# Feed-forward input in even-odd order, and norm factors moved into layer 1's key, value and query weights

## The chip, the core and the metric

One core of a Trainium2 chip runs the whole program. The metric is the device time of one execution in microseconds (us); the core's span in the profile is given beside it where both are known. TensorE (PE, and PEld for its weight loads) does the matmuls, VectorE (DVE) and ScalarE (ACT) the elementwise work, GpSimd (POOL) a little of it, and SyncE (SP) issues nearly all transfers.

## The reference

A trunk of two layers on 256 tokens of 1024 features, all in float32: layer 0 has attention over 16 heads, layer 1 has windowed attention with sinks over 16 query heads and 4 shared key/value heads, and each layer ends in a gated feed-forward block with a causal convolution of width 3. What the change touches, cut from the reference:

```python
def rmsnorm(x, g):
    y = x * rsqrt(mean(x * x, axis=-1) + EPS)
    return y * g
...
hk = rmsnorm(x, kv_norm)                       # layer 1
k, v = split(hk @ w_kv_b, 2)
h = rmsnorm(x, attn_norm[1])
q = partial_rope(heads(h @ w_q_b))
...
def conv_ffn(h, w_up, conv_w, conv_b, w_down): # both layers, h = rmsnorm(x, ffn_norm[l])
    u = h @ w_up                               # 1024 -> 2 * 2816
    u = conv_b + sum(conv_w[j] * shifted(u, j) for j in range(3))
    gate, val = split(u, 2)
    return (silu(gate) * val) @ w_down
```

A norm has two kinds of factors: one per token (the inverse root) and one per feature (`g`). The per-feature factor may stand at the input or at the rows of the weight matrix; the product is the same up to rounding.

## The kernel before

Tokens lie in two blocks of 128 (`b`), features in 8 chunks of 128 (`c`), which come in two halves of four (`n`). Every float32 operand of a projection is split in two parts: a rounded high part and the low part that is left. A product is then three matmuls: high x high, high x low, low x high.

**Weights.** They come in 92 units of 128 x 2048 numbers (1 MB each), in the order of their use. `fetch` loads a unit into one of three buffers `wr`; `prepare` splits it piece by piece: `hi_part` copies a piece to `wh` on ScalarE (L164), `lo_part` subtracts on VectorE and writes `wl` (L167). There are four buffers each of `wh` and `wl`, so unit i+4 is prepared when unit i has been used (`used`), and unit i+3 is fetched when unit i is split. The number of pieces `n` is 2 for most units (1024 wide) and 4 for some. Units 49 and 50 hold layer 1's key and value weights (`U_KV`), 51 to 54 its query weights (`U_QB`, each all 8 chunks of 256 columns), 55 on its output weights, 16 to 37 and 59 to 80 the two up projections.

**Order.** `chain` puts off small steps by an amount of planned time and `tick` runs those that are due while matmuls are written down; `require` runs what a matmul needs. From that order a list scheduler sets the order on each engine, except in stretches marked by hand.

**Features.** `feats` turns one block and half of the residual `xr` from tokens x features to features x tokens: four transposes on TensorE (L271) into two PSUM banks `t`, then per pair of chunks two ScalarE copies with the per-feature factor as scale (L283), a VectorE cast to the high part (L286) and a subtraction for the low part (L287). There are only two `t` banks, shared with other transposes. For the feed-forward block the scaled copy is kept as `y` (`keep`), because the per-token factors come later: the first four units of the up projection use the unscaled input and are scaled afterwards, while `scale_x` multiplies `y` by the row `rb` of token factors (L732) and splits it again (L734, L735) for the other 18 units. Between the layers (`after_f0`) `feats` makes two sets from the same transposes, `kT_h` with `kv_norm` and `qT_h` with `attn_norm[1]`, each with its own copies, casts and subtractions.

**Projections.** The up projection (L719 to L721) holds 128 x 128 weights and streams 256 tokens of one chunk; per unit it does 2 halves x 8 chunks x 3 products, for 22 units a layer. `proj` (L324 to L326) does it the other way round: it holds a block's features and streams weight columns, 512 for keys and values, 256 for queries. Its weights are packed on the host so that columns 0, 2, 4, ... of a group stand first and 1, 3, 5, ... behind, and a matmul reads them alternately from both halves:

```python
def turns(ap):
    return ap.rearrange("p (a t) -> p t a", a=2)
def pairs(ap):
    return ap.rearrange("p (t a) -> p t a", a=2)
...
nc.tensor.matmul(pairs(o), xh[:, blk(b)], turns(wh), start=(c == 0), stop=False)
```

After a projection of keys or queries, `rotate` copies the sums out with the token factor (L1046 for keys, L1059 for queries), applies the rotary embedding on VectorE (`rope`, L353 to L359), transposes on TensorE (L365) and splits the result (L376, L371). The attention then computes scores (L490 to L497).

Of the kernel before, what the change touches and what calls it, by code (L numbers as in the profile page):

```python
# [14 lines left out]
P = 128  # L15
# [45 lines left out]
def trunk(ctx: ExitStack, tc, x, xw, pos, cpk, fin, sinks, w, out):  # L61
# [96 lines left out]
    def fetch(i):  # L158
        if i < N_UNITS:
            raws[i] = wp.tile([P, UNIT], F32, tag="raw", name=f"wr{i}", bufs=3)  # L160
            nc.sync.dma_start(raws[i], w[i])

    def hi_part(i, c):
        nc.scalar.activation(wq[i][0][:, c], raws[i][:, c], AF.Copy)  # L164

    def lo_part(i, c):
        nc.vector.tensor_tensor(out=wq[i][1][:, c], in0=raws[i][:, c], in1=f(wq[i][0][:, c]), op=ALU.subtract)  # L167

# [4 lines left out]
    def prepare(i):  # L173

        if i >= N_UNITS:
            return
        n = 4 if i <= 5 or 1 <= i - U_UP0 <= 3 or 1 <= i - U_UP1 <= 3 or U_QB + 1 <= i <= U_OB else 2
        cut = [slice(k * UNIT // n, (k + 1) * UNIT // n) for k in range(n)]
# [84 lines left out]
    def new_hT():  # L263

        return [(quad(), quad()) for _ in range(2)]

    def feats(b, n, sets, key, keep=None):

# [6 lines left out]
        def steps(hT, g, y, m):  # L275
            c = slice(2 * m, 2 * m + 2)
            hi, lo = (part[:, c, blk(b)] for part in hT[n])
            y_ = y[:, c]

            def gain():  # L280
                for j in range(2):
                    col = g + 4 * n + 2 * m + j
                    nc.scalar.activation(y_[:, j], ts[m][:, j * P:(j + 1) * P], AF.Copy, scale=cp[:, col:col + 1])  # L283

            def parts():
                nc.vector.tensor_copy(hi, y_)  # L286
                nc.vector.tensor_tensor(out=lo, in0=y_, in1=f(hi), op=ALU.subtract)  # L287

            return gain, parts

        for k, (hT, g) in enumerate(sets):
            y = mid().rearrange("p (j t) -> p j t", j=4) if keep is None else keep[n][:, :, blk(b)]
            for m in range(2):
                gain, parts = steps(hT, g, y, m)
                chain(key, (200.0 + 1000.0 * k + 500.0 * m, gain), (500.0, parts))

    def square(b, n):
# [402 lines left out]
    def ffn(layer, u_up, u_dn, hT, y, rb, after, tail=None):  # L700
# [5 lines left out]
        def mm(i, up, cs_):  # L706
            need(u_up + i)
            hi, lo = wq[u_up + i]
            for j in range(2):
                o = up[j]  # L710
                for c in cs_:
# [5 lines left out]
                    s_ = slice((2 * c + j) * P, (2 * c + j + 1) * P)  # L717
                    xh, xl = hx(hT if i < n_raw else hS, c)
                    nc.tensor.matmul(o, hi[:, s_], xh, start=(c == 0), stop=False)  # L719
                    nc.tensor.matmul(o, hi[:, s_], xl, start=False, stop=False)  # L720
                    nc.tensor.matmul(o, lo[:, s_], xh, start=False, stop=(c == KC - 1))  # L721
                    tick(3 * 256 / 2.4)

        def scale_x(m):
# [4 lines left out]
            def times():  # L729
                for b in range(NB):  # L730
                    require("rb", b)
                nc.vector.tensor_tensor(out=y_, in0=y_, in1=rb.unsqueeze(1).to_broadcast([P, 2, S]), op=ALU.mult)  # L732

# [295 lines left out]
    o_down[0].finish(3, after_a, by_half=True)  # L1029
    kT_h = new_hT()  # L1030
    qT_h = new_hT()
    rs1 = []

    def after_f0(b, n):
        chain(("sq", b), (3000.0, lambda: square(b, n)))
        if n == 1:
            chain(("rs", b), (3000.0 + 700.0, lambda: rs1.append(rstd_of(b))))
        feats(b, n, [(kT_h, G_KV), (qT_h, G_ATTN1)], ("x", b, n))

# [10 lines left out]
    for b in range(NB):  # L1050
        o = bank("acc")
        run(proj(o, kT_h, b, cols512(U_KV), (U_KV, U_KV + 1) if b else ()))
        rotate(o, 2, b, kT[:, 0:2], kT[:, 2:4], ("qk", 0), lambda t, b=b, o=o: kv_out(t, b, o),
# [7 lines left out]
    def q_group(g):  # L1061
        q = quad()
        for b in range(NB):
            o = bank("acc")[:, :256]
            yield from proj(o, qT_h, b, cols256(U_QB + g), (U_QB + g,) if b else ())
            rotate(o, 2, b, q[:, 0:2], q[:, 2:4], ("qk", g), lambda t, b=b, o=o: q_out(t, b, o))
# [167 lines left out]
```

## Time and profile before

| | |
|---|---|
| three timed runs | 564.3, 564.4 and 563.48 us, median 564.3 |
| profiled execution | 563.05 us, its span 561.2 us |
| layer 0 | up projection from 116 to 238 us, down projection to 296 us |
| layer 1 | keys and values from 296 us, first queries from 308 us, scores from 318 us |
| layer 1's feed-forward block | up projection from 376 to 498 us, down projection to 553 us |

The profile lists each engine's busy time, idle times with what ended them, and the chain of work that ended last. A matmul's recorded duration overlaps that of its neighbours, so rates are read from starts.

### The profile page before, as it was taken

How to read it: one execution, taken by the hardware profiler on the slowest of the kernel's cores; microseconds unless marked ns; L12 is line 12 of the kernel's file. 1: busy time of each engine (PE TensorE's matmuls, PEld its weight loads, DVE VectorE, ACT ScalarE, POOL GpSimd, SP SyncE). 2: the span in 40 equal slices, each digit the busy share in tenths (PEclk: the TensorE clock that was granted, in tenths of full speed). 3: DMA queues.
4: the chain of work that ended last, by engine and by line, in shares of the span. 5: the costliest groups of instructions: out<-in, count | busy, mean ns of one | idle time of the engine just before them, and what ended most of it. 6: DMA issues, size and time to landing. Idle time of an engine off the chain costs nothing.

```text
span 561.2 us, 10529 instructions
## 1 busy us (share of the span) xinstructions
PE 548.0 (98%) x4022; PEld 510.9 (91%) x4022; DVE 439.1 (78%) x932; ACT 377.0 (67%) x767; POOL 107.3 (19%) x130
## 2 busy tenths in 40 slices
PE   9998999999999999999999999999999999999995
PEld 8997898899999999988888988889999999998884
DVE  6899988589798888764369988888898888874514
ACT  6759887779567777644349798887657777663313
POOL 8422202011422332100001000001332322210003
PEclk9999999999999999999999999999999999999998
DMA  8954464432466665566542724242465565656301
GB/s 320 375 200 171 151 227 149 151 131 96 161 221 221 226 223 193 192 222 220 203 172 88 289 76 151 75 151 76 151 221 204 200 211 217 239 205 224 121 0 75
DMA packets 15312, 101.00 MB, mean 180 GB/s; under 512 B 1952, under 2 KB 2080, under 8 KB 3744
## 3 DMA queue, kind: packets, MB, share of 16 engines
q1 hardware_dynamic: 14976, 100.09, 50.2%
q8 instruction: 31, 0.51, 0.4%
q10 hardware_dynamic: 288, 0.26, 0.1%
q14 instruction: 17, 0.14, 0.1%
HBM read 99.30 MB, written 1.05 MB: 179 GB/s over the span
## 4 chain that ended last, share of the span: by engine, by line
PE 81%; DVE 9%; ACT 4%; DMA 3%; issue 2%; POOL 0%; SPq 0%; DVEq 0%; POOLq 0%; ACTq 0%
PE acc L624 9%; PE acc L625 9%; PE acc L629 9%; PE u L721 6%; PE u L719 6%; PE u L720 6%; PE t L721 6%; PE t L719 6%; PE t L720 6%; DVE wl L167 4%; PE acc L720 2%; PE acc L719 2%; PE acc L721 2%; PE t L574 2%; DMA wr<-in_w 2%
## 5 line engine op out<-in xcount | busy, mean ns | idle before, releaser
L167 DVE TENSOR_TENSOR wl<-wr,wh 128x1024 fp32r<-128x1024 f32 (+1 forms) x208 | 223.4, 1090 | 59.6 <-ACT wh L164 59.0
L164 ACT ACTIVATE wh<-wr 128x1024 fp32r<-128x1024 f32 (+1 forms) x204 | 187.4, 951 | 62.6 <-PE acc L629 49.0
L763 POOL TENSOR_TENSOR m<-m,m 128x256 f32<-128x256 f32 x44 | 63.7, 1448 | 177.2 <-DVE m L758 126.1
L624 PE MATMUL acc<-wh,q 128*128 128x512 f32 x238 | 92.1, 387 | 0.0
L625 PE MATMUL acc<-wl,q 128*128 128x512 f32 x238 | 90.6, 380 | 0.0
L719 PE MATMUL u<-q,wh 128*128 128x256 f32 x320 | 88.4, 277 | 0.0
L720 PE MATMUL u<-q,wh 128*128 128x256 f32 x320 | 88.1, 276 | 0.0
L721 PE MATMUL u<-q,wl 128*128 128x256 f32 x320 | 88.0, 275 | 0.0
L721 PE MATMUL t<-q,wl 128*128 128x256 f32 x288 | 79.2, 275 | 0.0
L719 PE MATMUL t<-q,wh 128*128 128x256 f32 x288 | 79.2, 275 | 0.0
L720 PE MATMUL t<-q,wh 128*128 128x256 f32 x288 | 79.2, 275 | 0.0
L629 PE MATMUL acc<-wh,q 128*128 128x512 f32 x238 | 74.6, 379 | 0.0
L720 PEld LDWEIGHTS u<-q,wh 128*128 128x128 f32 x320 | 60.1, 188 | 0.0
L721 PEld LDWEIGHTS u<-q,wl 128*128 128x128 f32 x320 | 60.1, 188 | 0.0
L719 PEld LDWEIGHTS u<-q,wh 128*128 128x128 f32 x320 | 59.9, 188 | 0.0
L720 PEld LDWEIGHTS t<-q,wh 128*128 128x128 f32 x288 | 54.1, 188 | 0.0
L721 PEld LDWEIGHTS t<-q,wl 128*128 128x128 f32 x288 | 54.1, 188 | 0.0
L719 PEld LDWEIGHTS t<-q,wh 128*128 128x128 f32 x288 | 54.0, 188 | 0.0
L624 PEld LDWEIGHTS acc<-wh,q 128*128 128x128 f32 x238 | 45.0, 189 | 7.0 <-issue 0.7
L629 PEld LDWEIGHTS acc<-wh,q 128*128 128x128 f32 x238 | 45.0, 189 | 6.3
L625 PEld LDWEIGHTS acc<-wl,q 128*128 128x128 f32 x238 | 45.0, 189 | 5.9 <-issue 0.2
L767 ACT ACTIVATE q<-m 128x256 fp32r<-128x256 f32 x44 | 18.1, 416 | 38.5 <-POOL m L763 38.5
(188 smaller groups left out, 1131.2 us busy)
## 6 DMA issues: line engine op xcount, KB each, us to landing
wr<-in_w SPq DMA_DIRECT2D x90, 1024.0 KB, 4.8
first<-in_xw SPq DMA_DIRECT2D x5, 384.0 KB, 5.8
xr<-in_x SPq DMA_DIRECT2D x2, 512.0 KB, 8.2
first<-in_xw SPq DMA_DIRECT2D x1, 768.0 KB, 7.2
fin_t<-in_fin SPq DMA_DIRECT2D x1, 512.0 KB, 5.5
out<-ot SPq DMA_DIRECT2D x1, 512.0 KB, 2.6
first<-in_xw SPq DMA_DIRECT2D x1, 388.0 KB, 3.3
out<-m ACTq DMA_DIRECT2D x1, 256.0 KB, 2.1
```

The costliest lines, as they stand in the source:

```text
L164: nc.scalar.activation(wq[i][0][:, c], raws[i][:, c], AF.Copy)
L167: nc.vector.tensor_tensor(out=wq[i][1][:, c], in0=raws[i][:, c], in1=f(wq[i][0][:, c]), op=ALU.subtract)
L574: nc.tensor.matmul(o[:, P:] if kb else o, v_sb[kb][:, vcol(2 * j + e)], pT[p][e][:, S:] if kb else pT[p][e][:, :S], start=(kb == 0), stop= ...
L624: nc.tensor.matmul(pairs(o), ph[:, blk(b)], turns(hi[:, s_]), start=first, stop=False)
L625: nc.tensor.matmul(pairs(o), ph[:, blk(b)], turns(lo[:, s_]), start=False, stop=False)
L629: nc.tensor.matmul(pairs(o), pl[:, blk(b)], turns(hi[:, s_]), start=False, stop=end)
L719: nc.tensor.matmul(o, hi[:, s_], xh, start=(c == 0), stop=False)
L720: nc.tensor.matmul(o, hi[:, s_], xl, start=False, stop=False)
L721: nc.tensor.matmul(o, lo[:, s_], xh, start=False, stop=(c == KC - 1))
L763: nc.gpsimd.tensor_tensor(out=h, in0=gs, in1=t[1], op=ALU.mult)
L767: (3400.0, lambda: nc.scalar.activation(hi, h, AF.Copy)),
```

## The change

Two things are changed together.

First, the feed-forward input `hT`, `hS` and `y` is stored with even tokens first and odd tokens behind, for all 256 tokens of a chunk. `feats` with `keep` reads the transposed block from PSUM with a step of two and writes two runs of 64; `scale_x` reads `rb` with a step of two; the up projection reads its moving operand with `turns`, so its output stands in the order of before.

Second, between the layers `raw_feats` takes the place of `feats`: one set `xT_h` without a factor, for keys, values and queries, with one ScalarE copy and one VectorE subtraction for each pair of chunks, both straight from PSUM. The per-feature factors are applied when the weights are split: `hi_part` gets a scale and `lo_part` becomes a scalar_tensor_tensor (raw x factor - high part) for units 49 to 54. Since a factor belongs to one chunk, a piece may hold one chunk only: the key and value units are split in 4 pieces of 512 columns (before: 2), the query units in 8 pieces of 256 (before: 2 for the first, 4 for the others).

```diff
+    def factor(i, c):
+        if U_KV <= i < U_QB:
+            return cp[:, G_KV + 4 * (i - U_KV) + c.start // 512:][:, :1]
+        if U_QB <= i < U_OB:
+            return cp[:, G_ATTN1 + c.start // 256:][:, :1]
+        return None
+
     def hi_part(i, c):
-        nc.scalar.activation(wq[i][0][:, c], raws[i][:, c], AF.Copy)
+        g = factor(i, c)
+        nc.scalar.activation(wq[i][0][:, c], raws[i][:, c], AF.Copy, **({} if g is None else {"scale": g}))
 
     def lo_part(i, c):
+        g = factor(i, c)
+        if g is not None:
+            nc.vector.scalar_tensor_tensor(out=wq[i][1][:, c], in0=raws[i][:, c], scalar=g, in1=f(wq[i][0][:, c]),
+                                           op0=ALU.mult, op1=ALU.subtract)
+            return
         nc.vector.tensor_tensor(out=wq[i][1][:, c], in0=raws[i][:, c], in1=f(wq[i][0][:, c]), op=ALU.subtract)
...
-        n = 4 if i <= 5 or 1 <= i - U_UP0 <= 3 or 1 <= i - U_UP1 <= 3 or U_QB + 1 <= i <= U_OB else 2
+        n = 8 if U_QB <= i < U_OB else 4 if U_KV <= i < U_QB or i <= 5 or 1 <= i - U_UP0 <= 3 or 1 <= i - U_UP1 <= 3 or i == U_OB else 2
...
+    def evens(ap, b):
+        return ap.rearrange("p c (a t) -> p c a t", a=2)[:, :, :, b * P // 2:(b + 1) * P // 2]
+
     def feats(b, n, sets, key, keep=None):
...
-            hi, lo = (part[:, c, blk(b)] for part in hT[n])
-            y_ = y[:, c]
+            if keep is None:
+                hi, lo = (part[:, c, blk(b)] for part in hT[n])
+                y_ = y[:, c]
+            else:
+                hi, lo = (evens(part[:, c], b) for part in hT[n])
+                y_ = evens(y[:, c], b)
...
-                    nc.scalar.activation(y_[:, j], ts[m][:, j * P:(j + 1) * P], AF.Copy, scale=cp[:, col:col + 1])
+                    t = ts[m][:, j * P:(j + 1) * P]
+                    nc.scalar.activation(y_[:, j], t if keep is None else t.rearrange("p (t a) -> p a t", a=2), AF.Copy,
+                                         scale=cp[:, col:col + 1])
...
+    def raw_feats(b, n, hT, key):
+
+        ts = [bank("t"), bank("t")]
+        for j in range(4):
+            nc.tensor.transpose(ts[j // 2][:, (j % 2) * P:(j % 2 + 1) * P],
+                                xr[b][:, (4 * n + j) * P:(4 * n + j + 1) * P], ident)
+        tick(450)
+        for m in range(2):
+            hi, lo = (part[:, 2 * m:2 * m + 2, blk(b)] for part in hT[n])
+            t = ts[m][:, :S].rearrange("p (j t) -> p j t", j=2)
+            chain(key, (200.0 + 400.0 * m, lambda t=t, hi=hi: nc.scalar.activation(hi, t, AF.Copy)),
+                  (500.0, lambda t=t, hi=hi, lo=lo: nc.vector.tensor_tensor(out=lo, in0=t, in1=f(hi), op=ALU.subtract)))
...
-                    xh, xl = hx(hT if i < n_raw else hS, c)
-                    nc.tensor.matmul(o, hi[:, s_], xh, start=(c == 0), stop=False)
-                    nc.tensor.matmul(o, hi[:, s_], xl, start=False, stop=False)
-                    nc.tensor.matmul(o, lo[:, s_], xh, start=False, stop=(c == KC - 1))
+                    xh, xl = (turns(t) for t in hx(hT if i < n_raw else hS, c))
+                    nc.tensor.matmul(pairs(o), hi[:, s_], xh, start=(c == 0), stop=False)
+                    nc.tensor.matmul(pairs(o), hi[:, s_], xl, start=False, stop=False)
+                    nc.tensor.matmul(pairs(o), lo[:, s_], xh, start=False, stop=(c == KC - 1))
...
-                nc.vector.tensor_tensor(out=y_, in0=y_, in1=rb.unsqueeze(1).to_broadcast([P, 2, S]), op=ALU.mult)
+                y4 = y_.rearrange("p c (a t) -> p c a t", a=2)
+                r4 = rb.rearrange("p (t a) -> p a t", a=2).unsqueeze(1).to_broadcast([P, 2, 2, P])
+                nc.vector.tensor_tensor(out=y4, in0=y4, in1=r4, op=ALU.mult)
...
-        feats(b, n, [(kT_h, G_KV), (qT_h, G_ATTN1)], ("x", b, n))
+        raw_feats(b, n, xT_h, ("x", b, n))
```

`proj` reads `xT_h` where it read `kT_h` and `qT_h`. On TensorE the order of the matmuls is as before, apart from the transposes between the layers. On VectorE, at the first rotation of keys (L353 before, L391 now; `m2` is the copied sum, `wl51` to `wl53` are low parts of query units, `q_156` and `q_157` parts of the features), before:

```order
L167 TENSOR_TENSOR wl51_3623<-wr51_3451,wh51_3622 128x1024
L286 CAST q_156_1526<-m2_330_3649 128x2x128 x2
L287 TENSOR_TENSOR q_157_1527<-m2_330_3649,q_156_1526 128x2x128 x2
L167 TENSOR_TENSOR wl52_3687<-wr52_3483,wh52_3686 128x512
L308 TENSOR_TENSOR st_331_3653<-st_331_3653 128x1
L353 TENSOR_TENSOR rb_94<-m2_334_3697,cs_255 128x64
L309 TENSOR_SCALAR st_331_3653<-st_331_3653 128x1
L358 TENSOR_TENSOR rb_94<-m2_334_3697,sn_256 128x4x8 x2
L167 TENSOR_TENSOR wl52_3687<-wr52_3483,wh52_3686 128x512
L359 TENSOR_TENSOR m2_334_3697<-rb_94 128x4x16
```

and now:

```order
L178 SCALAR_TENSOR_TENSOR wl51_3595<-wr51_3447,cp_83,wh51_3594 128x256
L178 SCALAR_TENSOR_TENSOR wl52_3639<-wr52_3501,cp_83,wh52_3638 128x256
L178 SCALAR_TENSOR_TENSOR wl51_3595<-wr51_3447,cp_83,wh51_3594 128x256
L178 SCALAR_TENSOR_TENSOR wl52_3639<-wr52_3501,cp_83,wh52_3638 128x256
L391 TENSOR_TENSOR rb_94<-m2_322_3648,cs_255 128x64
L396 TENSOR_TENSOR rb_94<-m2_322_3648,sn_256 128x4x8 x2
L178 SCALAR_TENSOR_TENSOR wl52_3639<-wr52_3501,cp_83,wh52_3638 128x256
L397 TENSOR_TENSOR m2_322_3648<-rb_94 128x4x16
```

The casts and subtractions of the features no longer stand ahead of the rotation; pieces of unit 52 do, of which more are done by then. On ScalarE, from the squares of the last block (L301 before, L339 now) to the copy of the keys' sums (L1046 before, L1085 now), before:

```order
L301 ACTIVATE m2_332_3654,st_331_3653<-xr1_93 128x512
L283 ACTIVATE m2_329_3648<-t_327_3642,cp_83 128x128 x2
L283 ACTIVATE m2_329_3648<-t_328_3643,cp_83 128x128 x2
L164 ACTIVATE wh51_3622<-wr51_3451 128x1024
L283 ACTIVATE m2_330_3649<-t_327_3642,cp_83 128x128 x2
L283 ACTIVATE m2_330_3649<-t_328_3643,cp_83 128x128 x2
L164 ACTIVATE wh52_3686<-wr52_3483 128x512
L301 ACTIVATE m2_333_3691,st_331_3653<-xr1_93 128x512
L1046 ACTIVATE m2_334_3697<-acc_326_3615,rstd_324_3605 128x256
```

and now:

```order
L339 ACTIVATE m2_321_3641,st_319_3614<-xr1_93 128x512
L332 ACTIVATE q_152_1522<-t_317_3608 128x2x128
L332 ACTIVATE q_152_1522<-t_318_3609 128x2x128
L173 ACTIVATE wh51_3594<-wr51_3447,cp_83 128x256
L173 ACTIVATE wh52_3638<-wr52_3501,cp_83 128x256
L173 ACTIVATE wh51_3594<-wr51_3447,cp_83 128x256
L173 ACTIVATE wh52_3638<-wr52_3501,cp_83 128x256
L173 ACTIVATE wh51_3594<-wr51_3447,cp_83 128x256
L173 ACTIVATE wh52_3638<-wr52_3501,cp_83 128x256 x2
L1085 ACTIVATE m2_322_3648<-acc_316_3589,rstd_314_3579 128x256
```

The last pair of `t` banks is read by two copies where eight stood, and pieces of two query units alternate ahead of the keys' copy.

More of the change, by code (lines that the diff above doesn't have):

```diff
@@ L291, in feats @@
         for k, (hT, g) in enumerate(sets):
-            y = mid().rearrange("p (j t) -> p j t", j=4) if keep is None else keep[n][:, :, blk(b)]
+            y = mid().rearrange("p (j t) -> p j t", j=4) if keep is None else keep[n]
             for m in range(2):
@@ L1029, in trunk @@
     o_down[0].finish(3, after_a, by_half=True)
-    kT_h = new_hT()
-    qT_h = new_hT()
+    xT_h = new_hT()
     rs1 = []
@@ L1051, in trunk @@
         o = bank("acc")
-        run(proj(o, kT_h, b, cols512(U_KV), (U_KV, U_KV + 1) if b else ()))
+        run(proj(o, xT_h, b, cols512(U_KV), (U_KV, U_KV + 1) if b else ()))
         rotate(o, 2, b, kT[:, 0:2], kT[:, 2:4], ("qk", 0), lambda t, b=b, o=o: kv_out(t, b, o),
@@ L1064, in q_group @@
             o = bank("acc")[:, :256]
-            yield from proj(o, qT_h, b, cols256(U_QB + g), (U_QB + g,) if b else ())
+            yield from proj(o, xT_h, b, cols256(U_QB + g), (U_QB + g,) if b else ())
             rotate(o, 2, b, q[:, 0:2], q[:, 2:4], ("qk", g), lambda t, b=b, o=o: q_out(t, b, o))
```

## The prediction

> **What bounds the kernel now.** I read the head of the page and its chain of waits first.
>
> ```profile
> span 561.2 us, 10529 instructions
> PE 548.0 (98%) x4022; PEld 510.9 (91%) x4022; DVE 439.1 (78%) x932; ACT 377.0 (67%) x767; POOL 107.3 (19%) x130
> PE 81%; DVE 9%; ACT 4%; DMA 3%; issue 2%; POOL 0%; SPq 0%; DVEq 0%; POOLq 0%; ACTq 0%
> ```
>
> TensorE carries 81% of the chain that ends last, VectorE and ScalarE together 13%. So anything that shortens the stream of matmuls shows in the time, and the other engines count only where TensorE waits for them. The windows tell the two kinds of stage apart; columns are busy time and count of PE, PEld, DVE, ACT and POOL, the granted clock, the DMA share and GB/s.
>
> ```profile
> 140.00:180.00 40.00, 40.00 (x355) 40.00 (x354) 34.22 (x56) 25.25 (x42) 13.06 (x7) 1.00 0.57 203
> 440.00:480.00 40.00, 40.00 (x355) 40.00 (x355) 34.35 (x58) 29.47 (x49) 12.72 (x8) 1.00 0.61 216
> 280.00:286.00 6.00, 6.00 (x30) 5.25 (x29) 3.07 (x3) 2.82 (x4) 0.00 (x0) 1.00 0.62 228
> 290.00:296.00 6.00, 5.98 (x33) 4.67 (x32) 5.16 (x20) 5.74 (x22) 0.00 (x0) 1.00 0.28 116
> 296.00:304.00 8.00, 7.82 (x39) 6.56 (x39) 7.96 (x24) 8.00 (x25) 0.55 (x1) 1.00 0.06 9
> 304.00:309.00 5.00, 4.88 (x30) 4.13 (x29) 5.00 (x14) 5.00 (x12) 2.55 (x5) 1.00 0.66 241
> ```
>
> In the up projections of both layers (first two rows) TensorE never stops, at the full granted clock, while VectorE is 86% busy and DMA 0.6: the matmul's own rate is the limit. From 290 to 309 us, where layer 0 hands over to layer 1, ScalarE is busy 18.7 of 19 us and VectorE 18.1 of 19, and TensorE can wait for them.
>
> How fast the matmuls really follow each other is read from starts, since the recorded 275 ns of one overlaps its neighbours.
>
> ```profile
> 199.98 0.28 PE L719 MATMUL t<-q,wh 128*128 128x256 f32 x1
> ...
> 205.76 0.28 PE L719 MATMUL u<-q,wh 128*128 128x256 f32 x1
> ```
>
> Between these two lie 51 steps: 5.78 us / 51 = 113.3 ns for each 256 columns read straight through. The same size read alternately from two halves exists already, in layer 1's query projection, and so does the 512-column form in the value projection:
>
> ```profile
> 308.06 0.28 PE L326 MATMUL acc<-wh,q 128*128 128x256 f32 x1
> ...
> 310.07 0.28 PE L326 MATMUL acc<-wh,q 128*128 128x256 f32 x1
> ```
>
> ```profile
> 62.10 0.38 PE L326 MATMUL acc<-wh,q 128*128 128x512 f32 x1
> ...
> 66.63 0.38 PE L326 MATMUL acc<-wh,q 128*128 128x512 f32 x1
> ```
>
> 18 steps take 2.01 us, 111.7 ns each; 21 steps of 512 take 4.53 us, 215.7 ns each. Straight reading thus costs 1.6 ns more per matmul of 256.
>
> **The change, part 1: the feed-forward input.** The up projection issues 22 units x 2 halves x 8 chunks x 3 products = 1056 matmuls of 256 columns a layer, 2112 in all, every one of which now reads its moving operand as the query projection does (two runs of 128 elements, one element from each in turn). Priced by the two rows: 2112 x 1.6 ns = 3.4 us, all on the path, since TensorE is solid there. Bounds: nothing gained if the 111.7 belongs to streaming weights rather than to the reading; at most 2112 x (113.3 - 107.9) = 11.4 us, if a 256-column matmul took half of the 215.7. I take 111.7 because it is the same size, stride and output pattern; only the roles of weights and activations are swapped.
>
> [...]
>
> What pays for it is where the input is written. ScalarE now takes its columns from PSUM with a step of two, VectorE writes runs of 64, and the scaling by the row factors reads these with a step of two. Nothing is added in number. The nearest rows are today's own:
>
> ```profile
> L283 ACT ACTIVATE y<-t,cp 128x128 f32<-128x128 f32 x32 | 9.4, 411 | 0.2
> 116.41 0.48 PE L719 MATMUL u<-q,wh 128*128 128x256 f32 x2
> 120.89 0.42 DVE L287 TENSOR_TENSOR q<-y,q 128x256 fp32r<-128x256 f32 x1
> ```
>
> I cost it at nothing: the last part of the input is ready at 121.3 us, and before it is needed stand 48 matmuls of the first four chunks, from 116.4 us on, 48 x 113.3 ns = 5.4 us, so until 121.8 without the transposes between them. If a step of two doubled the streaming part of these ScalarE copies (128 columns, at most some 0.15 us each by the 0.29 us that one occupies), the 16 of a layer would come 2.4 us late at the end and TensorE would lose up to 1.9 us a layer; were they quicker, nothing would come of it.
>
> **Part 2: the factors move into the weights.** Costs are busy time over count, since neighbours overlap by their tails.
>
> ```profile
> L283 ACT ACTIVATE m<-t,cp 128x128 f32<-128x128 f32 x32 | 9.4, 419 | 4.1 <-PE t L271 4.0
> L286 DVE CAST q<-m 128x256 fp32r<-128x256 f32 x16 | 4.3, 288 | 0.8 <-ACT m L283 0.8
> L287 DVE TENSOR_TENSOR q<-m,q 128x256 fp32r<-128x256 f32 x16 | 6.3, 420 | 0.1
> L376 ACT ACTIVATE q<-t 128x256 fp32r<-128x256 f32 x10 | 3.8, 376 | 0.0
> L371 DVE TENSOR_TENSOR q<-t,q 128x256 fp32r<-128x256 f32 x10 | 4.2, 418 | 0.3 <-ACT q L376 0.3
> L164 ACT ACTIVATE wh<-wr 128x1024 fp32r<-128x1024 f32 x152 | 157.2, 1052 | 59.9 <-PE acc L629 47.2 <-PE t L720 6.0 <-PE u L720 4.4
> L167 DVE TENSOR_TENSOR wl<-wr,wh 128x1024 fp32r<-128x1024 f32 x152 | 186.2, 1237 | 53.3 <-ACT wh L164 53.0
> L164 ACT ACTIVATE wh<-wr 128x512 fp32r<-128x512 f32 x52 | 30.2, 654 | 2.7 <-PE acc L629 1.8 <-DMA wr<-in_w 1.0
> L167 DVE TENSOR_TENSOR wl<-wr,wh 128x512 fp32r<-128x512 f32 x56 | 37.1, 692 | 6.2 <-ACT wh L164 6.0
> L536 ACT ACTIVATE m<-m,hst 128x256 f32<-128x256 f32 x32 | 14.3, 497 | 0.0
> L882 DVE SCALAR_TENSOR_TENSOR q<-first,g,q 128x256 fp32r<-128x256 f32 x6 | 2.9, 479 | 1.2 <-ACT q L876 1.2
> ```
>
> Features: 32 scaled copies (9.4 us of ScalarE), 16 casts and 16 subtractions (10.6 us of VectorE) go. Eight plain copies at 0.38 us (3.0) and eight subtractions at 0.42 us (3.4) come. Query weights: two pieces of 1024 and twelve of 512 become 32 of 256. ScalarE paid 2 x 1.03 + 12 x 0.58 = 9.0 us and pays 32 x 0.45 = 14.3 (a 256-wide copy with a scale per partition, as at L536); VectorE paid 2 x 1.23 + 12 x 0.66 = 10.4 and pays 32 x 0.48 = 15.5. Key and value weights: four pieces of 1024 become eight of 512. A scale cost 0.07 us on ScalarE (0.45 against 0.38) and 0.06 on VectorE (0.48 against 0.42), so each new piece is 0.65 and 0.72 us: 1.1 us more on ScalarE (8 x 0.65 - 4 x 1.03) and 0.9 on VectorE (8 x 0.72 - 4 x 1.23). They lie at 280 to 286 us, where both engines are half idle under the down projection, and cost nothing; without that cover TensorE would wait 1.1 us at the first key matmul.
>
> The totals hardly move: ScalarE -9.4 + 3.0 + 5.3 + 1.1 = 0.0 us, VectorE -10.6 + 3.4 + 5.1 + 0.9 = -1.2 us. What moves is the order: copies that TensorE waits for are fewer and come earlier, weight pieces that it needs later fill up behind. What is there to win:
>
> ```profile
> PEld t L271 <- ACT m L283: 1.2, 3, 0.6
> PEld t L365 <- ACT wh L164: 0.9, 2, 0.5
> PEld t L365 <- issue: 0.3, 1, 0.3
> 297.83 0.38 PE L326 MATMUL acc<-wh,q 128*128 128x512 f32 x1
> 298.39 0.44 PE L271 MATMUL t<-ident,xr 128*128 128x128 f32 x2 [0.18 <-ACT m L283]
> ```
>
> These are TensorE's waits from 286 to 320 us: 2.4 us of weight loads. The stream loses less than a load's wait, because the matmul ahead still runs: at 297.83 the next start came 0.56 us later instead of 0.22, a loss of 0.34 for the longest wait of 0.6. Scaled so, 2.4 us of waits are about 1.4 us of path. The first row goes: a pair of PSUM banks was held for eight copies, 8 x 0.29 = 2.4 us, and is now for two copies and the last subtraction, 2 x 0.38 + 0.42 = 1.2. The second row is VectorE reaching the keys' rotation late; the weight pieces ahead of it for the first block shrink with the removed casts, but for the queries the 1.2 us per unit that the eighths add (8 x 0.48 against 4 x 0.66) stand in the same queue, so the 0.3 stays. I take 1.0 us; bounds are 1.4 gained, and 5.3 lost if all that the query weights add to ScalarE stood before something awaited. Then the attention's scores would be late, and the softmax behind them.
>
> **Sum.** 3.4 + 1.0 = 4.4 us. The profiled execution took 563.05 us around its 561.2 us span; the three timed runs have a median of 564.3, 1.25 more. The four runs' middle is 563.9, and I subtract from that: 559.5 us.
>
> **Rivals.** (A) The forecast: 559.5; by its own bounds 558 to 561.
>
> (B) The reading gains nothing. Every matmul that runs at 111.7 streams weights and holds activations; every one at 113.3 does the opposite. If that is the cause, the up projections stay: 563.9 - 1.0 = 562.9. For it: no row of the trace separates the two. Against: the sizes of both operands are the same in both.
>
> (C) The gap between matmuls falls further, towards half of the 512-column step: 2112 x 5.4 ns + 1.0 = 12.4 us, 551.5. Against it stands the query projection, which doesn't get there. [...]
>
> (D) Slower: the query weights in eighths make the scores late. ScalarE is full from 290 to 309 us, and 5.3 us are added to these units; if they all end up before the rotation that the transposes wait for, 563.9 - 3.4 + 5.3 = 565.8. It decides from 3.4 us of delay on. Against it: the removed copies free more than that in the same 19 us.
>
> [...]
>
> **How the numbers follow.** A 0.60, B 0.15, C 0.12, D 0.08, E 0.05. The time is A's, 559.5. The range reaches up to B and down halfway towards C, 555 to 563.4; left out are most of C, half of D and E, less than 2 in 10. 0.2% is 1.1 us, about what a measurement of this kernel can tell from no change. Faster: A, C, a part of B and a mild D, 0.80. Same: the rest of B and some of D, 0.12. Slower: E and a full D, 0.08.
>
> **What would show it.** The up projection's matmuls start 111.7 ns apart and each up stage is 1.7 us shorter; the waits of the transposes on ScalarE vanish between 286 and 300 us, and the scores of layer 1 start about 2.7 us earlier than at 318.25 (1.7 of the first up stage, 1.0 of the hand-over). I am wrong if that step stays at 113.3 or passes 114, if TensorE shows waits on the new feature copies near 119 and 379 us, or if the transposes of keys and queries wait longer than now.

## Result and profile after

| | before | after |
|---|---|---|
| median of the runs made side by side | 563.89 us (563.12 to 564.4) | 559.01 us (558.19 to 559.24) |
| ratio, 95% interval | | 0.9906 [0.9891, 0.9921] |
| profiled execution and its span | 563.05 and 561.2 us | 559.24 and 557.2 us |

The change makes the kernel 4.9 us faster; 559.5 was predicted. The head of the page after and its chain of waits:

```profile
span 557.2 us, 10523 instructions
PE 543.3 (97%) x4022; PEld 507.3 (91%) x4022; DVE 435.8 (78%) x930; ACT 376.7 (68%) x765; POOL 115.1 (21%) x130
PE 76%; DVE 10%; ACT 5%; DMA 5%; issue 2%; POOL 0%; SPq 0%; DVEq 0%; POOLq 0%; ACTq 0%
```

TensorE's busy time fell by 4.7 us at the same 4022 matmuls. The windows that answer to those of before (same columns, each stretch 2 us earlier; in this execution the first up projection begins 1.35 us later than before and the scores of layer 1 begin 2.14 us earlier):

```profile
138.00:178.00 40.00, 40.00 (x361) 40.00 (x360) 34.29 (x56) 26.14 (x45) 12.55 (x6) 1.00 0.52 190
438.00:478.00 40.00, 40.00 (x361) 40.00 (x360) 34.58 (x57) 29.49 (x49) 12.42 (x8) 1.00 0.60 211
278.00:284.00 6.00, 6.00 (x30) 5.25 (x29) 2.74 (x4) 2.81 (x5) 0.00 (x0) 1.00 0.60 187
288.00:294.00 6.00, 6.00 (x33) 5.04 (x32) 3.65 (x12) 3.09 (x9) 0.55 (x1) 1.00 0.48 175
294.00:302.00 8.00, 8.00 (x43) 7.02 (x42) 7.15 (x21) 8.00 (x24) 0.72 (x1) 1.00 0.01 2
302.00:307.00 5.00, 5.00 (x29) 4.42 (x28) 4.56 (x15) 4.33 (x13) 1.39 (x3) 1.00 0.80 288
```

In 40 us of an up projection lie 361 matmuls instead of 355 (those that an edge cuts are counted). In the hand-over between the layers (last three rows) TensorE is busy in all of 19 us; before, its rows there summed to 18.68, and VectorE (15.36 of 19 us) and ScalarE (15.42) are no longer full in the same stretch except for ScalarE from 294 to 302.

The rate of the up projection, first and last of 57 starts:

```profile
199.74 0.28 PE L757 MATMUL t<-q,wh 128*128 128x256 f32 x1
...
205.99 0.28 PE L759 MATMUL u<-q,wl 128*128 128x256 f32 x1
```

6.25 us / 56 = 111.6 ns a step, against 113.3. Where the stages begin is read from the first matmul of each: up projection, down projection, keys and values, queries, scores, second up and down projection. After:

```profile
117.76 0.47 PE L757 MATMUL u<-q,wh 128*128 128x256 f32 x2
...
236.92 0.38 PE L662 MATMUL acc<-wh,q 128*128 128x512 f32 x1
...
295.40 0.38 PE L362 MATMUL acc<-wh,q 128*128 128x512 f32 x1
...
306.42 0.27 PE L362 MATMUL acc<-wh,q 128*128 128x256 f32 x1
...
316.11 0.29 PE L528 MATMUL acc<-kd,q 128*128 128x256 f32 x1
...
374.29 0.48 PE L757 MATMUL u<-q,wh 128*128 128x256 f32 x2
...
493.45 0.38 PE L662 MATMUL acc<-wh,q 128*128 128x512 f32 x1
```

and those of them in the kernel before that the prediction does not show:

```profile
237.38 0.38 PE L624 MATMUL acc<-wh,q 128*128 128x512 f32 x1
...
296.02 0.46 PE L324 MATMUL acc<-wh,q 128*128 128x512 f32 x1
...
307.84 0.27 PE L324 MATMUL acc<-wh,q 128*128 128x256 f32 x1
...
318.25 0.28 PE L490 MATMUL acc<-kd,q 128*128 128x256 f32 x1
...
376.41 0.49 PE L719 MATMUL u<-q,wh 128*128 128x256 f32 x2
...
497.39 0.38 PE L624 MATMUL acc<-wh,q 128*128 128x512 f32 x1
```

| from the first matmul of ... to that of ... | before | after | difference |
|---|---|---|---|
| up 0, down 0 | 120.97 | 119.16 | -1.81 |
| down 0, keys and values | 58.64 | 58.48 | -0.16 |
| keys and values, queries | 11.82 | 11.02 | -0.80 |
| queries, scores | 10.41 | 9.69 | -0.72 |
| scores, up 1 | 58.16 | 58.18 | +0.02 |
| up 1, down 1 | 120.98 | 119.16 | -1.82 |

So 3.63 us come from the two up projections and 1.68 from the hand-over, 5.3 together. The profiled spans differ by 4.0 only, because this execution of the changed kernel reached its first up projection 1.35 us later (117.76 against 116.41). That lies in work which the change does not touch, behind a weight transfer; in the chain of waits after, which before has no transfer at that time, it stands as

```profile
51.44 7.64 DMA wr<-in_w
```

Profiled executions differ there without regard to the edit: layer 0's output projection starts at 86.46 us before, at 87.81 after, and in the experiments below between 86.47 and 89.55 (the last section says what differs). Kernels are therefore compared here by the time from that projection's first matmul to the end of the span: 474.74 us before, 469.43 after, 5.31 less.

The waits of TensorE's weight loads from 284 to 318 us are one wait now, where seven stood. Six of them are in the rows that the prediction shows; the seventh is `PEld t L271 <- issue: 0.3, 1, 0.3`. Now:

```profile
PEld t L326 <- DVE q L333: 0.3, 1, 0.3
```

### The profile page after: what moved, and what is told of

Its sections match the earlier page's. It is cut to its first block, busy times and chain, and to the rows that moved or that the text cites. A ratio compares the mean times of both kernels' runs of the same rounds, so it can differ in the third digit from the quotient of the medians.

```text
span 557.2 us, 10523 instructions
## 1 busy us (share of the span) xinstructions
PE 543.3 (97%) x4022; PEld 507.3 (91%) x4022; DVE 435.8 (78%) x930; ACT 376.7 (68%) x765; POOL 115.1 (21%) x130
## 4 chain that ended last, share of the span: by engine, by line
PE 76%; DVE 10%; ACT 5%; DMA 5%; issue 2%; POOL 0%; SPq 0%; DVEq 0%; POOLq 0%; ACTq 0%
PE acc L662 9%; PE acc L663 9%; PE acc L667 9%; PE u L758 6%; PE u L757 6%; PE u L759 6%; PE t L758 6%; PE t L757 6%; PE t L759 6%; DMA wr<-in_w 4%; DVE wl L181 3%; PE acc L757 2%; PE acc L759 2%; PE acc L758 2%; PE t L612 2%
## 5 line engine op out<-in xcount | busy, mean ns | idle before, releaser
L181 DVE TENSOR_TENSOR wl<-wr,wh 128x1024 fp32r<-128x1024 f32 (+1 forms) x190 | 208.1, 1111 | 49.5 <-ACT wh L173 49.2
L173 ACT ACTIVATE wh<-wr 128x1024 fp32r<-128x1024 f32 (+1 forms) x186 | 174.4, 964 | 52.0 <-PE acc L667 42.3
L803 POOL TENSOR_TENSOR m<-m,m 128x256 f32<-128x256 f32 x44 | 72.7, 1653 | 164.8 <-DVE m L798 99.3
L759 PEld LDWEIGHTS u<-q,wl 128*128 128x128 f32 x320 | 61.4, 192 | 0.0
L758 PEld LDWEIGHTS u<-q,wh 128*128 128x128 f32 x320 | 61.4, 192 | 0.0
L757 PEld LDWEIGHTS u<-q,wh 128*128 128x128 f32 x320 | 61.3, 192 | 0.0
L757 PEld LDWEIGHTS t<-q,wh 128*128 128x128 f32 x288 | 55.3, 192 | 0.0
L758 PEld LDWEIGHTS t<-q,wh 128*128 128x128 f32 x288 | 55.3, 192 | 0.0
L759 PEld LDWEIGHTS t<-q,wl 128*128 128x128 f32 x288 | 55.3, 192 | 0.0
```

The lines of the kernel that those rows point to most:

```text
L173: nc.scalar.activation(wq[i][0][:, c], raws[i][:, c], AF.Copy, **({} if g is None else {"scale": g}))
L757: nc.tensor.matmul(pairs(o), hi[:, s_], xh, start=(c == 0), stop=False)
L758: nc.tensor.matmul(pairs(o), hi[:, s_], xl, start=False, stop=False)
L759: nc.tensor.matmul(pairs(o), lo[:, s_], xh, start=False, stop=(c == KC - 1))
L803: nc.gpsimd.tensor_tensor(out=h, in0=gs, in1=t[1], op=ALU.mult)
```

## Experiments

First the two parts of the change, each alone.

**Reading only.** Up projection as in the changed kernel; between the layers `feats` with two sets, factors and pieces as before.

```diff
-    xT_h = new_hT()
+    kT_h = new_hT()
+    qT_h = new_hT()
...
-        raw_feats(b, n, xT_h, ("x", b, n))
+        feats(b, n, [(kT_h, G_KV), (qT_h, G_ATTN1)], ("x", b, n))
```

> Only the feed-forward input is stored even tokens first and read alternately; between the layers the two sets of features and the old weight pieces stay. Theory (two separate gains, 3.6 us in the up projections, 1.7 us at the hand-over): the up projection's matmuls start 111.7 ns apart, the hand-over from 290 to 318 us is as before, 560.3 us. Rival (the parts need each other, because faster matmuls in layer 0 only run into the hand-over's waits): 562 us or more.

560.36 us (559.5 to 560.98), ratio 0.9931 [0.9915, 0.9947] to 564.1 for the kernel before. The up stages are 1.82 and 1.81 us shorter, from the first down projection to the scores nothing changes, and the waits of the hand-over are those of before:

```profile
PEld t L291 <- ACT m L308: 1.2, 3, 0.6
PEld t L404 <- ACT wh L174: 0.9, 2, 0.5
```

Part 1 is worth 3.6 us in the trace by itself.

**Factors only.** The feed-forward input in token order, read straight; the rest as in the changed kernel.

```diff
-                    xh, xl = (turns(t) for t in hx(hT if i < n_raw else hS, c))
+                    xh, xl = hx(hT if i < n_raw else hS, c)
```

> Only the factors move into the weights and the features become raw; the feed-forward input stays in natural order and is read straight. Theory: up projection steps of 113.3 ns, first scores 1.7 us earlier than before, 562.2 us. Rival (the query weights in eighths cost what the removed copies save): 563.9 us, no change.

562.49 us (560.81 to 563.55), ratio 0.9971 [0.9959, 0.9982]. Up stages as before, the hand-over 1.68 us shorter. Counted from layer 0's output projection to the end the two halves give -3.63 and -1.64 us, together the -5.31 of the whole change within 0.1: the parts don't touch each other.

**Stored by turns, read straight.** The input is written even tokens first as in the changed kernel, and the up projection takes it in stored order, so the block behind it sees the tokens in that order.

```diff
-                    xh, xl = (turns(t) for t in hx(hT if i < n_raw else hS, c))
-                    nc.tensor.matmul(pairs(o), hi[:, s_], xh, start=(c == 0), stop=False)
+                    xh, xl = hx(hT if i < n_raw else hS, c)
+                    nc.tensor.matmul(o, hi[:, s_], xh, start=(c == 0), stop=False)
```

> The changed kernel, its feed-forward input stored even tokens first, but read straight through; the tokens then stand in the wrong order in the feed-forward block, which is left so. Theory (the order of reading makes the step): 113.3 ns, and the time of factors alone, 562.2 us. Rival (the stored order, or where the tiles lie, makes it): 111.7 ns, 559 us. If the writing side costs anything, waits on the new copies near 119 and 377 us show here too.

563.12 us (561.47 to 564.21), ratio 0.9981 [0.9968, 0.9994]. First and last of 56 starts:

```profile
199.75 0.28 PE L758 MATMUL t<-q,wh 128*128 128x256 f32 x1
...
205.99 0.28 PE L759 MATMUL u<-q,wl 128*128 128x256 f32 x1
```

6.24 / 55 = 113.5 ns. The order in which the matmul reads makes the step, not where the data lie. From layer 0's output projection to the end it takes 473.12 us, against 473.10 for the factors alone: the writing by turns costs nothing.

**Weights read straight.** The other way round: all projections that stream weights read them straight from weights packed in natural order, while the feed-forward input is still read by turns.

```diff
     def turns(ap):
+        return ap.rearrange("p (t a) -> p t a", a=2)
...
-        return m.reshape(*s[:-1], s[-1] // n, n // 2, 2).swapaxes(-1, -2).reshape(s)
+        return m
```

> The changed kernel, but the weights that are streamed (values, keys, queries, output and down projections) are packed in natural order and read straight; the feed-forward input is read alternately. Theory with a loss per matmul: 512-column steps go from 215.7 to 217.4 ns, 858 of them and 192 query matmuls, 1.8 us, 560.8 us. With a loss per element: 219.1 ns, 3.2 us, 562.2 us. Rival (only streamed activations care for the order): 215.7 ns, 559 us.

567.1 us (565.99 to 567.83), ratio 1.005 [1.0032, 1.0067]: slower than the kernel before. The expected size was missed. In layer 0's value projection, first and last of 16 starts:

```profile
63.48 0.39 PE L365 MATMUL acc<-wh,q 128*128 128x512 f32 x1
...
66.88 0.39 PE L365 MATMUL acc<-wh,q 128*128 128x512 f32 x1
```

3.40 / 15 = 226.7 ns, 11 ns above the 215.7 by turns, where 1.7 to 3.4 were expected. Straight reading costs 226.7 / 512 = 0.443 ns per column and 113.3 / 256 = 0.443 as well: at these two lengths its step goes with the columns. By turns 512 columns take 0.421 ns each, but 256 take 0.436: there, as I read it, something other than the stream holds the step. The 714 matmuls of 512 columns in the output and down projections (three groups of 238, as the page counts them) would give 714 x 11 ns = 7.9 us. Their stages are 7.1 us longer than in the changed kernel, layer 1's attention with its later queries included; from layer 1's keys to its first scores it is 1.0 us longer; together 8.1 us, counted from layer 0's output projection to the end.

The queries, 256 columns, don't keep to the 113.3. Their first 24 steps take about that, later ones more, for example over 20 starts:

```profile
313.34 0.28 PE L367 MATMUL acc<-wh,q 128*128 128x256 f32 x1
...
315.59 0.28 PE L365 MATMUL acc<-wh,q 128*128 128x256 f32 x1
```

2.25 / 19 = 118.4 ns, where the same matmuls by turns take 111 to 112. What adds these 5 ns to the straight reading was not sought.

**Without the factors.** As the changed kernel, with the factors `kv_norm` and `attn_norm[1]` left out and the weight pieces of before, to see what scaling and small pieces cost.

```diff
-        if U_KV <= i < U_QB:
-            return cp[:, G_KV + 4 * (i - U_KV) + c.start // 512:][:, :1]
...
+        return None
...
-        n = 8 if U_QB <= i < U_OB else 4 if U_KV <= i < U_QB or i <= 5 or ...
+        n = 4 if i <= 5 or ... or U_QB + 1 <= i <= U_OB else 2
```

> The changed kernel without the factors of keys, values and queries (left out altogether) and with the weight pieces of before (2 of 1024, 4 of 512). Theory (the eighths and the scaling are hidden; the whole gain of the hand-over comes from the removed copies): the same as the changed kernel, 559.0 us, first scores near 316 us. Rival (they are paid for on the path): up to 1 us faster, 558 us.

558.23 us (557.71 to 558.85), ratio 0.9896 [0.9881, 0.991], within the interval of the changed kernel's, though the median is nearer to the rival's 558. The traces speak against the rival: from layer 0's output projection to the end it takes 469.56 us against 469.43, from the first down projection to the scores 79.37 against 79.19. Where the two profiled executions differ is ahead of that point, where the edit does not act (86.47 us here, 87.81 in the changed kernel). The scaling of the pieces and their number are hidden, and the removed copies, casts and subtractions alone bring 1.50 of the 1.68 us (80.87 to 79.37). Which of them TensorE had been waiting behind was not separated.

**Small pieces only.** The kernel before, with the changed kernel's pieces (4 for keys and values, 8 for queries).

```diff
-        n = 4 if i <= 5 or 1 <= i - U_UP0 <= 3 or 1 <= i - U_UP1 <= 3 or U_QB + 1 <= i <= U_OB else 2
+        n = 8 if U_QB <= i < U_OB else 4 if U_KV <= i < U_QB or i <= 5 or 1 <= i - U_UP0 <= 3 or 1 <= i - U_UP1 <= 3 or i == U_OB else 2
```

> The kernel before with the new pieces alone (4 for keys and values, 8 for queries), no factors in them, both sets of features. It adds 4.1 us of ScalarE and 3.0 us of VectorE work to a hand-over where both are full. Theory: without the removed copies as cover the rotations come late and the first scores are 1 to 3 us later than before, 565 to 567 us. Rival (there is slack for it, so the eighths never mattered): 564 us.

564.03 us (563.35 to 566.97), ratio 1.0004 [0.9988, 1.0021]. I had expected a loss of one to three microseconds and was wrong. The trace shows two opposite movements. Smaller pieces let the rotation in earlier, and the scores start 1.03 us sooner after the first down projection than in the kernel before (79.84 against 80.87 us). All of it is given back before the next group's scores, which start 14.98 us after the first ones, against 13.96 in the kernel before; for example where the score products (L497) wait for the split of the queries:

```profile
PEld u L497 <- DVE q L371: 0.4, 1, 0.4
```

I read this as two full engines: with two sets of features VectorE and ScalarE have next to no room (18.1 and 18.7 of 19 us busy from 290 to 309 us in the kernel before), and smaller pieces only move the wait to a later place. With one set (16.2 and 16.4 of 19 us in the same window of the changed kernel) the gain is still there at the second scores and up to the end.

Then three on what reading by turns is. All of them are the changed kernel with another order of the feed-forward input.

**Pairs and quarters.** Two neighbouring tokens are taken from each half in turn, or one token from each of four quarters.

```diff
-                    xh, xl = (turns(t) for t in hx(hT if i < n_raw else hS, c))
+                    xh, xl = (t.rearrange("p (a t e) -> p t a e", a=2, e=2) for t in ...)   # pairs
+                    xh, xl = (t.rearrange("p (a t) -> p t a", a=4) for t in ...)            # quarters
```

> The changed kernel with two neighbouring tokens at a time from each half instead of one. [...]

> The changed kernel with the input stored in four quarters (token mod 4) and read in turn from each, so that the same stretch comes up every fourth element only. If distance between accesses to one stretch matters, less than 111.7 ns a step and up to 5 us faster; if something else holds the matmuls at 111.7, the same step, 559 us.

670.35 and 613.84 us, one run each. Neither time was expected. First and last of 39 starts of the pairs, and of 46 of the quarters:

```profile
199.73 0.34 PE L758 MATMUL u<-q,wh 128*128 128x256 f32 x1
...
205.98 0.34 PE L757 MATMUL t<-q,wh 128*128 128x256 f32 x1
```

```profile
199.70 0.30 PE L757 MATMUL u<-q,wh 128*128 128x256 f32 x1
...
205.93 0.30 PE L757 MATMUL t<-q,wh 128*128 128x256 f32 x1
```

6.25 / 38 = 164.5 ns and 6.23 / 45 = 138.4 ns: both far slower than straight reading, though with pairs the reading changes runs only half as often as with single elements.

**Near halves.** One token from each of two runs again, but the runs lie 64 elements apart (even and odd tokens of one block of 128) instead of 128, in a pattern of three dimensions as the pairs have.

```diff
-                    xh, xl = (turns(t) for t in hx(hT if i < n_raw else hS, c))
+                    xh, xl = (t.rearrange("p (b a t) -> p b t a", b=2, a=2) for t in hx(hT if i < n_raw else hS, c))
```

> The changed kernel, with the even-odd order made within each block of 128 tokens, so that a matmul still takes one element from each of two runs in turn, but the runs lie 64 elements (256 bytes) apart instead of 128 (512 bytes); four runs in turn at 64 elements distance had taken 136 to 142 ns a step. Theory, number of runs: two runs in turn are enough whatever their distance, and the four runs were slow because there were four: 111.7 ns, 559 to 560 us. Rival, distance: 256 bytes between two reads that follow each other is what made the four runs slow: 125 to 142 ns, 588 to 620 us. Rival, a pattern with three dimensions costs by itself (the pairs, also of three dimensions, took 164.5 ns): 150 to 165 ns, 640 to 670 us.

559.98 us, one run; first and last of 56 starts:

```profile
199.75 0.28 PE L757 MATMUL t<-q,wh 128*128 128x256 f32 x1
...
205.89 0.28 PE L758 MATMUL u<-q,wh 128*128 128x256 f32 x1
```

6.14 / 55 = 111.6 ns. Neither the distance of 64 elements nor a third dimension is by itself what made quarters and pairs slow. Of the patterns tried, only one element from each of two runs is quicker than straight reading; why four runs or pairs are slower stays open.

**What holds the step at 111.6.** In the changed kernel and in the factors-only kernel, the two small products (high x low and low x high) use 64 of the 128 weight columns, so half of their output rows are left out.

```diff
-                    nc.tensor.matmul(pairs(o), hi[:, s_], xl, start=False, stop=False)
-                    nc.tensor.matmul(pairs(o), lo[:, s_], xh, start=False, stop=(c == KC - 1))
+                    nc.tensor.matmul(pairs(o[:64]), hi[:, h_], xl, start=False, stop=False)
+                    nc.tensor.matmul(pairs(o[:64]), lo[:, h_], xh, start=False, stop=False)
```

> The changed kernel, with the two small products (high x low, low x high) of the up projections computed for the first 64 of each 128 output rows only: two of every three matmuls load 64 weight columns instead of 128 and stream the same 256 tokens, alternately; the other half of these products is left out. Theory, load: alternate reading takes away what the stream cost over its 512-column rate, and what holds the 256-column step at 111.7 ns is the weight load that each matmul needs (the load's busy time equals the window's). Then two thirds of the steps fall to half of the 512-column step, 107.9 ns, or to somewhat above it, the mean step to between 109.2 and 110.5, and the time to between 553.7 and 556.5 us (2112 x 1.2 to 2.5 ns less than 559.0). Rival, fixed cost: a matmul of 256 columns has a fixed cost per instruction that does not depend on the load: 111.7 ns as before, 559.0. Rival, narrower loads are slower in some way that no run here has shown: a step above 112.

> The factors-only kernel (feed-forward input in token order, read straight, 113.3 ns a step, 562.5 us), again with the two small products of the up projections computed for the first 64 of each 128 output rows only; with alternate reading the steps of these narrow matmuls had fallen from 111.7 to 109.2 ns and the time to 556.1. Theory, two limits: a step is the slower of the stream (straight 0.4425 ns a column, so 113.3 for 256) and of something that goes with the held width (111.7 for 128 columns, 109.2 for 64); straight reading is held by the stream, so the width changes nothing: 113.3 ns, 562 to 563 us. Rival, two costs that add up: the narrow steps fall by 2.5 ns as they did with alternate reading, 110.8 ns, and the time by 2112 x 2/3 x 2.5 ns = 3.5 us to 559.0.

By turns 556.08 us, straight 563.33, one run each. First and last of 57 starts by turns, and of 56 straight:

```profile
199.79 0.28 PE L759 MATMUL t<-q,wh 128*128 128x256 f32 x1
199.90 0.27 PE L760 MATMUL t<-q,wh 128*64 128x256 f32 x1
200.01 0.27 PE L761 MATMUL t<-q,wl 128*64 128x256 f32 x1
...
205.95 0.27 PE L761 MATMUL u<-q,wl 128*64 128x256 f32 x1
```

```profile
199.75 0.28 PE L759 MATMUL u<-q,wh 128*128 128x256 f32 x1
...
205.99 0.28 PE L760 MATMUL t<-q,wh 128*64 128x256 f32 x1
```

6.16 / 56 = 110.0 ns by turns, 6.24 / 55 = 113.5 straight. Over all records by turns, a narrow matmul is followed after 109.1 ns and a wide one after 111.8 (medians 109 and 112). I read this as two limits, of which the slower one sets the step: the stream, 113.3 straight and at most 109.1 by turns, and something that goes with the 128 columns held, 111.7. Straight reading lies above both widths and doesn't feel them (113.3 and 113.5). The narrow step did not reach half of the 512-column step (107.9) as I had also allowed for. The next matmul's load is narrow behind a wide one too, and still the step is 111.9, so the limit goes with the matmul's own width; whether its load or its output rows make it was not separated.

**Layer 0's queries and keys too.** The changed kernel, with layer 0's query and key projections reading one token from each of the two blocks in turn, put back in order by VectorE's reads behind them. It was meant as a better version.

```diff
-                nc.tensor.matmul(om, wh, xh, start=(c == 0), stop=False)
+                xh, xl = turns(xh), turns(xl)
+                nc.tensor.matmul(pairs(om), wh, xh, start=(c == 0), stop=False)
...
-            nc.vector.tensor_tensor(out=t3, in0=o3, in1=c_, op=ALU.mult)
+            nc.vector.tensor_tensor(out=t4, in0=o4, in1=c_, op=ALU.mult)
```

> The changed kernel, and layer 0's query and key projections read their 256 moving tokens alternately too: the two token blocks lie next to each other as before, the projection takes token 0 of the first, token 0 of the second, token 1 of the first and so on, and the rotation's VectorE reads put the order back (a step of two in PSUM and in the copied sums). Theory: 8 chunks x 3 products x 16 groups = 384 matmuls fall from 113.3 to 111.7 ns, 0.6 us: 558.4 us, ratio to the kernel before about 0.990. Rival 1, the stage waits for VectorE or ScalarE and not for the stream: 559.0. Rival 2, the VectorE reads with a step of two are slower and make the stage longer: 559.5 to 561.

559.42 us (558.29 to 560.46), ratio 0.9915 [0.9897, 0.9932]: no better than the changed kernel's 0.9906, and between the two rivals. The steps do fall to 111 to 112 ns. But TensorE waits in this stage for the split of the weights, first in the changed kernel and then in this one,

```profile
PEld acc L488 <- DVE wl L181: 2.4, 2, 2.2
```

```profile
PEld acc L491 <- DVE wl L181: 3.1, 2, 2.7
```

and from 45 to 60 us VectorE is busy without a gap, as it is in the kernel before (15.00 us both; 14.12 in the changed kernel). TensorE's granted clock was 0.89 there, against 1.00 in the same stretch of the changed kernel's profile:

```profile
45.00:60.00 15.00, 13.57 (x100) 13.33 (x100) 15.00 (x39) 12.78 (x31) 1.58 (x2) 0.89 0.49 161
```

Layer 0's output projection starts 0.1 us sooner than in the changed kernel (87.71 against 87.81). From 47.3 to 50.5 us fifteen of the steps take 213 to 215 ns, some 1.5 us more than at 112. Because of that the profile doesn't tell whether the longer wait, the VectorE reads with a step of two or the clock took the 0.6 us; the runs show only that no gain is left.

## Why the prediction was right

**The bound.** That TensorE's stream of matmuls sets the time of the up stages, and the other engines only that of the hand-over, held: reading alone changed nothing but the up stages (1.82 and 1.81 us), the factors nothing but the hand-over (1.68 us).

**Part 1, 3.4 us: 3.63 measured.** The 1.6 ns came from two pairs of rows read to 0.01 us; over 57 starts it is 1.7 ns (113.3 to 111.6), and the measured 3.63 us are 1.72 ns for each of the 2112. Pricing by the query projection, where weights and activations change roles, was right. Rival B, which held the roles responsible, is refuted by both sides: tokens by turns take 111.6, and weights read straight take longer than by turns (226.7 against 215.7 at 512 columns, 113.3 to 118 against 111.7 at 256). Rival C, a gap that falls further, is refuted by 111.6 in the trace; the narrow matmuls (109.1 with 64 columns held, against 111.7 with 128) suggest why: with 128 a limit stands above the stream.

**Rival E, slower by alternate reading with the weights held,** is refuted for single elements from two runs: they take 111.6 ns, straight reading 113.3. That some patterns cost much more is true: 138.4 for quarters, 164.5 for pairs.

**The writing side, costed at nothing:** right. Stored by turns and read straight is as long as the factors alone to 0.02 us, and the rate of the up stage, transposes included, is the same in both.

**Part 2, 1.0 us: 1.68 measured, above its bound of 1.4.** The mechanism was as written: the waits of the feature transposes on ScalarE vanished, and the key and value pieces, now from 278.6 to 287 us, cost nothing (no wait of TensorE there). The mis-sized term is the scaling of the waits. I took 2.4 us of load waits times 0.34 / 0.6, the one place where I had read the start itself, and the fourth row of that view (L271 <- issue, 0.3) was left out. One of the late starts is that of the transposes of the first keys. Here it is with the matmul ahead of it, before and after:

```profile
305.37 0.38 PE L324 MATMUL acc<-wh,q 128*128 128x512 f32 x1
305.87 0.41 PE L365 MATMUL t<-ident,m 128*128 128x128 f32 x2
...
304.04 0.38 PE L364 MATMUL acc<-wh,q 128*128 128x512 f32 x1
304.25 0.38 PE L403 MATMUL t<-ident,m 128*128 128x128 f32 x2
```

Read from all starts, the first transpose of a group came 187, 108, 61, 347, 285, 373 and 288 ns later than the plain step, 1.65 us; after, 113 and 83 ns are left, 0.20. The transposes right behind a late one lost another 0.28 us, now 0.06. These two differences, 1.45 and 0.22, make up the 1.68. That the four transposes of a block and half mostly stand together now, where they came as two and two, brings nothing. In a group each step between transposes takes 109 ns, the step back to a matmul 28, and the matmul behind it 83 more than usual: 438 ns for one group of four, 440 for two of two. The second failed step is that "the 0.3 stays" for the queries because of the eighths: it went too. The pieces of the query units were priced well: by busy time over count, as the prediction reckons, 425 and 434 ns, where 450 and 480 were estimated:

```profile
L173 ACT ACTIVATE wh<-wr,cp 128x256 fp32r<-128x256 f32 x32 | 13.6, 504 | 0.7 <-ACT wh L173 0.7
L178 DVE SCALAR_TENSOR_TENSOR wl<-wr,cp,wh 128x256 fp32r<-128x256 f32 x32 | 13.9, 494 | 1.6 <-ACT wh L173 1.6
```

An awaited step can also stand behind a weight piece. Before, a piece of 512 (0.69 us) lay between the last two steps of the first keys' rotation on VectorE, now one of 256 (0.48 us). Small pieces alone brought the scores 1.03 us forward, although they add work. Beside the removed work this is worth little: with the old pieces and no factors the hand-over is 0.18 us longer.

**Rival D, the eighths make the scores late,** is refuted: without factors and eighths the hand-over is no shorter (79.37 against 79.19 us).

**The announced signs.** Step 111.7 and 1.7 us per up stage: 111.6 and 1.8. The scores 2.7 us before 318.25: they start 2.14 earlier at 316.11, and 3.5 earlier once the late start of this execution (1.35 us) is taken off. Of the signs of being wrong, TensorE's waits on the new feature copies near 119 us grew a little, before and after:

```profile
PEld t L271 <- ACT y L283: 0.5, 2, 0.3
PEld t L290 <- ACT y L307: 0.6, 3, 0.3
```

In layer 1 they went from 0.4 to 0.6 us. Stored by turns and read straight has 0.5 and 0.4 as before, so the copies are not what is slower; I read the rest as the faster matmuls reaching the transposes sooner, which was not separated. The up stages' 1.8 us each are net of this.

Sum: 5.3 us between the traces where 4.4 was forecast, 4.9 between the medians; two terms were small in the same direction, by 0.2 and 0.7. That the median comes within 0.5 us of the forecast is in part luck: the medians of the kernel before, in the sets of runs used here, lie between 563.89 and 564.38.

## What to carry to other kernels

Where TensorE never stops, read the step between matmul starts, not their recorded length (111.6 ns against 0.28 us here), and compare it for each access pattern that the kernel already has: a pattern that exists elsewhere in the trace priced the reading at 3.4 us, where 3.63 were measured, as long as the size was the same (256 columns did not price 512: 1.7 ns against 11), and a factor of 2112 makes 1.7 ns worth a change of layout. Where an engine waits for another's queue, count the lost starts at every wait rather than scaling the sum of waits, and ask what stands ahead of the awaited instruction: here the removed copies, casts and subtractions mattered far more than the length of the weight pieces (1.50 us against 0.18). In layer 0's attention, where TensorE waits for another engine, the same faster step brought nothing measurable (559.42 us against 559.01); what swallowed it is not shown.

## What the hardware showed

- A 256-column step in this kernel takes 113.3 ns read straight, 111.6 one element from each of two runs in turn (64 or 128 elements apart), 138.4 from four runs, 164.5 with pairs from two runs. At 512 columns straight costs 226.7 and by turns 215.7. I had expected the loss at 512 to be like that at 256; it is 11 ns against 1.7. Weights read straight at 256 columns took 113.3 at first and about 118 later.
- By turns a step also depends on the held width, 111.7 with 128 columns and 109.1 with 64; straight it does not (113.3 and 113.5).
- GpSimd's multiply of 128 x 256 in the feed-forward block (44 of them, L763 before, L803 after) changed with TensorE's reading though nothing in it was edited. Before and after:

```profile
L763 POOL TENSOR_TENSOR m<-m,m 128x256 f32<-128x256 f32 x44 | 63.7, 1448 | 177.2 <-DVE m L758 126.1 <-ACT m L762 29.9 <-ACT m L752 13.6
L803 POOL TENSOR_TENSOR m<-m,m 128x256 f32<-128x256 f32 x44 | 72.7, 1653 | 164.8 <-DVE m L798 99.3 <-ACT m L792 41.5 <-ACT m L802 23.9
```

  All four kernels with full-width straight reading have 1447 or 1448 ns, those by turns 1559 to 1662, quarters 1132, pairs 927; straight with half-width products it is 1550, so the reading alone does not set it. It costs nothing here, since no wait of TensorE in either kernel is on GpSimd, and its cause was not sought.
- Profiled executions of the same start-up differ by up to 3 us (86.46 to 89.55 us to layer 0's output projection), nearly as much as part 1 is worth; stages have to be compared by their own first matmuls. Six of the fourteen, all at 87.57 us or later, have a second weight transfer near 52 us in the chain of waits; in two more (reading only, near halves, 87.8) the first one takes about 11 us, against 9.2 in the kernel before. Four have a granted clock of 0.89 from 45 to 60 us (factors only, stored by turns, small pieces, layer 0 too). What each is worth was not separated.
